# Six eighths of one output store moved from SyncE's queue to GpSimd's, in transfers of 5, 121 and 2 partitions

## The chip, the cores and the metric

The kernel runs on one core of one Trainium2 chip. The metric is the device time of one execution in microseconds, lower being better. Times of a kernel come from repeated runs; a profile is one execution with every instruction and every DMA packet recorded.

## The reference

The computation is a batch of 128 independent matrix products in float32:

```python
b1, b2, m, k, n = 8, 16, 256, 512, 384
x      = np.random.randn(b1, b2, m, k).astype(np.float32)
weight = np.random.randn(b1, b2, k, n).astype(np.float32)
np.matmul(x, weight).astype(np.float32)      # (8, 16, 256, 384)
```

67 MB of x and 101 MB of weights are read, 50 MB of output are written, and nothing is used twice.

## The kernel before

The 128 products are worked off in 32 groups (NG) of four (G). A group is 1024 rows of x, four weight matrices and 1024 rows of output. In SBUF one group's x lies as 128 partitions of R = 8 rows each, so that every partition holds 16 KB that are contiguous in memory; its output lies in the same way, as 128 partitions of 8 rows of 384 float32, 12 KB that are contiguous. Weights of a group are one load of 24 KB for each partition, or two loads of 12 KB in the first four and the last two groups (`is_short`).

There is no scheduler: each engine has its program written out by hand, and semaphores order them.

- SyncE (`on_sync`) issues every DMA, all on one queue: for each group the load of x (`load_x`), the store of the group four earlier (`store`; LAG = 4), and the load of the weights (`load_w`). A load waits until the casts of two groups earlier have freed its buffer, a store until its output is copied (`o_copied`). After the last weights the stores of groups 27 to 31 follow. The store of group 26, the sixth last, is issued between the loads of x and of the weights of group 30.
- VectorE (`on_vector`) casts x to bfloat16 (`cast_x`) and most of the weights (`cast_w`, or `cast_short` in the short groups).
- TensorE (`on_tensor`) transposes x through the identity matrix and multiplies; ScalarE (`on_scalar`) copies the transposes out of PSUM (`evacuate`), casts the rest of the weights, and copies the products out (`copy_out`), four copies to a group (T = 4), into one of four output slots (OS). Before the first copy into a slot it waits for the store of the group four earlier.
- GpSimd (`on_gpsimd`) makes the identity matrix at the start and does nothing else.

The last stores differ in their semaphores: those of groups 28 to 30 count on `o_end`, that of group 31 on `o_fin`. SyncE waits for both at its end. Groups below 28 count on one of two semaphores `o_out`. The last group has its own layout (`is_full`), with packets of 3 KB in its store and 4 KB in its load of x.

In the profile's lines, L118 is the load of x, L135 the load of weights, L157 the store, L171 the cast of x, L184 and L200 the casts of weights in long and short groups, L275 the copy of the products.

Of the kernel before, what the change touches and what calls it, by code (L numbers as in the profile page):

```python
# [12 lines left out]
def kernel(  # L13
# [9 lines left out]
    b1, b2, M, K = x.shape  # L23
    _, _, _, N = weight.shape
# [5 lines left out]
    o_rows = out.rearrange("b1 b2 m n -> (b1 b2 m) n")  # L30
# [10 lines left out]
    G = 4  # L41
    C = P // G
    R = G * M // P
    T = R // 2
    SH, SL = 2, 4
    NG = B // G

    XS, WS, OS = 2, 2, 4
# [3 lines left out]
    LAG = 4  # L52
# [6 lines left out]

    PAD = 12  # L60

    ctx.enter_context(tc.tile_critical(sync_engine=mybir.EngineType.Pool, no_gpsimd_drain=True))  # L62

    def sbuf(name, shape, dtype, n):
        return [
            ctx.enter_context(nc.sbuf_tensor(f"{name}{s}", shape, dtype)) for s in range(n)
        ]
# [6 lines left out]
    def sems(name, n):  # L74
        return [tc.alloc_semaphore(f"{name}{s}") for s in range(n)]
# [9 lines left out]
    out_sb = sbuf("out_sb", [P, OS * R, N], fp32, 1)[0]  # L85
# [6 lines left out]
    id_done, x_cast, w_vcast, w_acast, t_made, t_copied, p_made, o_copied = (  # L92
        sems(name, 1)[0]
        for name in (
            "id_done", "x_cast", "w_vcast", "w_acast",
            "t_made", "t_copied", "p_made", "o_copied",
        )
    )
    x_in, w_in, o_out = sems("x_in", XS), sems("w_in", WS), sems("o_out", 2)
    h_in = sems("h_in", G)  # L100
    o_end = sems("o_end", 1)[0]
    o_fin, spare = sems("o_fin", 1)[0], sems("spare", 1)[0]

    BIAS = 8
# [17 lines left out]
    def is_full(n):  # L123
        return isinstance(n, int) and n == NG - 1
# [17 lines left out]
    def store(e, t, U, s, pieces=1):  # L142
        n = t * U + s
        dram = o_rows[bass.ds(n * (G * M), G * M)].rearrange("(p r) n -> p r n", r=R)
        if is_full(n):
            dram = o_rows[n * G * M : (n + 1) * G * M].rearrange("(i p r) n -> p i r n", i=G, p=P)
        for q in range(pieces):
            rows = slice(q * R // pieces, (q + 1) * R // pieces)
            last = isinstance(n, int) and n >= NG - OS
            if not last and (not isinstance(n, int) or n >= 2):  # L150
                e.wait_ge(o_out[s % 2], (t * (U // 2) + s // 2) * 16 + 16)
            e.wait_ge(o_copied, n * T + ((q + 1) * T // pieces + BIAS))
            src = out_sb[:, bass.ds(slot(t, U, s) * R + q * R // pieces, R // pieces)]
            if is_full(n):
                src = src.rearrange("p (i r) n -> p i r n", i=G)
                rows = slice(0, G)
            e.dma_start(out=dram[:, rows], in_=src).then_inc(  # L157
                o_fin if last and n == NG - 1 else o_end if last else o_out[s % 2], 16
            )

    def slot(t, U, s):
        return (t * U + s) % OS
# [106 lines left out]
    def copy_out(e, t, U, s, q):  # L269
        n = t * U + s  # L270
        if q == 0:
            if not isinstance(n, int) or n >= OS:
                e.wait_ge(o_out[s % 2], (t * (U // 2) + s // 2) * 16 + (16 - OS // 2 * 16 + 16))
        e.wait_ge(p_made, n * T + (q + 1 + BIAS))
        e.copy(  # L275
            out=out_sb[:, bass.ds(slot(t, U, s) * R + 2 * q, 2), :],
            in_=po[(s * T + q) % PO][:, :, :N],
        ).then_inc(o_copied, 1)

    def on_gpsimd(e):  # L280
        e.memset(identity[:], 0.0).then_inc(id_done, 1)  # L281
        e.wait_ge(id_done, 1)
        make_identity(nc, identity[:], nomemset=True)
        e.drain().then_inc(id_done, 1)

    def on_sync(e):
        U = 2
        for n in range(LAG):
            load_x(e, 0, NG, n)
            load_w(e, 0, NG, n)  # L290
        rounds = (NG - 2 - LAG) // U
        with e.Fori(0, rounds) as t:
            for s in range(U):
                load_x(e, t, U, LAG + s)
                store(e, t, U, s)
                load_w(e, t, U, LAG + s)

        for n in range(LAG + rounds * U, NG):
            load_x(e, 0, NG, n)
            if n < NG - 1:  # L300
                store(e, 0, NG, n - LAG)
            load_w(e, 0, NG, n)
        for n in range(NG - 1 - LAG, NG):
            store(e, 0, NG, n)
        e.wait_ge(o_end, 16 * (OS - 1))
        with e.Fori(0, 4):
            e.sem_inc(spare, 1)
        for _ in range(PAD):
            e.sem_inc(spare, 1)
        e.wait_ge(o_fin, 16)  # L310
# [46 lines left out]
    def on_scalar(e):  # L357
# [8 lines left out]
        def step(t, U, s):  # L366
            short = is_short(t * U + s + 1)
            evacuate(e, t, U, s + 1, range(T - 1))
            for q in range(T):
                copy_out(e, t, U, s, q)  # L370
                if q == 0:
                    evacuate(e, t, U, s + 1, range(T - 1, T))
                if q == 0 and short:
                    e.sem_inc(w_acast, CA)
                if q > 0 and not short:
                    last = CA if q == T - 1 else q
                    cast_w(e, t, U, s + 1, range(CV + q - 1, CV + last), q == 1)
# [11 lines left out]
        for q in range(T):  # L389
            copy_out(e, 0, NG, NG - 1, q)  # L390

    on_gpsimd(nc.gpsimd)
    on_sync(nc.sync)
    on_vector(nc.vector)
# [32 lines left out]
```

## Time and profile before

| | before |
|---|---|
| median of 3 runs | 517.65 us (517.05 to 517.83) |
| the profiled execution | 517.57 us |
| its span, first to last instruction | 515.8 us |
| DVE busy | 397.7 us (77%) |
| ACT busy | 409.7 us (79%) |
| PE busy | 320.0 us (62%) |
| POOL busy | 0.7 us (0%) |
| DMA moved | 218.18 MB at a mean of 423 GB/s |
| store of a group | 1536.0 KB, median 25.0 us from issue to landing |

DVE is VectorE, ACT ScalarE, PE TensorE, POOL GpSimd, SP SyncE. The span is cut into 40 slices in the page, and each digit of a row is the busy share of a slice in tenths, 9 standing for 90% or more; the row DMA is the mean over the core's 16 DMA engines. A time from issue to landing includes the queue that stood ahead. In a timeline, a line gives start, length, engine, source line, operation and tiles, the number of instructions, and in brackets the idle time before with what ended it.

### The profile page before, as it was taken

To read this page: it belongs to the slowest core of one execution; us is meant where nothing else is said; L and a number is where in the kernel's file an instruction comes from. 1 tells how busy PE (TensorE), PEld (TensorE's weight loads), DVE (VectorE), ACT (ScalarE), POOL (GpSimd) and SP (SyncE) were. 2 spreads that over 40 slices of the span, in tenths; PEclk is the share of its full clock that TensorE was granted. 3 is DMA by queue.
4 is the path that set the end of the run, shared out by engine and by line. 5 is a ranking of instruction groups with operands and counts; after the bars stand their busy time and mean duration, and the time that the engine had idled before them with its cause. 6 is when DMAs were issued, how large, how long until landed. Compare 5 with 4: busy or idle time off the path is not lost.

```text
span 515.8 us, 11659 instructions
## 1 busy us (share of the span) xinstructions
PE 320.0 (62%) x4512; PEld 222.0 (43%) x4512; DVE 397.7 (77%) x462; ACT 409.7 (79%) x387; POOL 0.7 (0%) x6
## 2 busy tenths in 40 slices
PE   2276737567586656675655864767657477656871
PEld 2254425444354443453443543535445354434550
DVE  2788757788777897777977778877789777797960
ACT  1365577798978997987998799889798978997751
POOL 0000000000000000000000000000000000000000
PEclk9698878677866877876888686778667876877697
DMA  8999999999999999999999999999999999999996
GB/s 337 428 423 426 437 430 420 435 431 433 431 424 432 430 439 428 429 426 432 433 436 428 423 434 431 437 429 425 430 431 434 433 429 427 430 435 423 421 429 250
DMA packets 15462, 218.18 MB, mean 423 GB/s; under 512 B 1632, under 2 KB 1632, under 8 KB 2656
## 3 DMA queue, kind: packets, MB, share of 16 engines
q1 hardware_dynamic: 15456, 218.11, 99.3%
q8 instruction: 3, 0.05, 0.0%
q14 instruction: 3, 0.02, 0.0%
HBM read 167.77 MB, written 50.33 MB: 423 GB/s over the span
## 4 chain that ended last, share of the span: by engine, by line
DMA 57%; DVE 29%; issue 9%; PE 1%; DVEq 1%; SPq 1%; ACT 0%; POOLq 0%
DMA w_sb<-in_weight_dram 57%; DVE w_bf L184 20%; DVE x_bf L171 5%; DVE w_bf L200 4%; PE po L260 1%; SPq L135 0%; DVEq L334 0%; SPq L118 0%; DVEq L62 0%; DVEq L180 0%; ACT out_sb L275 0%; SPq L130 0%; DVEq L168 0%; DVEq L194 0%; SPq L422 0%
## 5 line engine op out<-in xcount | busy, mean ns | idle before, releaser
L184 DVE CAST w_bf<-w_sb 32x1536 bf16<-32x1536 f32 x286 | 271.9, 951 | 81.1 <-DMA w_sb<-in_weight_dram 73.0
L242 PE MATMUL po<-w_bf,x_t 128*32 128x384 bf16 x3968 | 201.5, 364 | 33.4 <-DVE w_bf L184 25.4
L224 PE MATMUL pt<-identity,x_bf 128*128 128x128 f32 x512 | 113.5, 409 | 149.1 <-DVE x_bf L171 149.1
L184 ACT CAST w_bf<-w_sb 32x1536 bf16<-32x1536 f32 x130 | 191.0, 1470 | 5.1 <-DMA w_sb<-in_weight_dram 1.9
L224 PEld LDWEIGHTS pt<-identity,x_bf 128*128 128x128 f32 x512 | 101.3, 223 | 161.5 <-issue 161.0
L242 PEld LDWEIGHTS po<-w_bf,x_t 128*32 128x32 bf16 x3968 | 117.7, 107 | 116.3 <-issue 51.5
L275 ACT COPY out_sb<-po 128x768 f32 (+1 forms) x128 | 102.5, 800 | 59.7 <-PE po L242 53.9
L211 ACT COPY x_t<-pt 128x1024 bf16<-128x1024 bf16 x128 | 123.6, 1021 | 20.9 <-PE pt L224 20.3
L171 DVE CAST x_bf<-x_sb 128x1024 bf16<-128x1024 f32 x128 | 80.0, 688 | 12.5 <-DMA x_sb<-in_x_dram 11.7
L200 DVE CAST w_bf<-w_sb 64x1536 bf16<-64x1536 f32 x48 | 45.8, 955 | 8.3 <-DMA w_sb<-in_weight_dram 7.0
L211 ACT ACT_TABLE_LOAD x1 | 1.3, 1283 | 10.8 <-PE pt L224 10.8
L260 PE MATMUL po<-w_bf,x_t 128*128 128x384 bf16 x32 | 5.4, 326 | 2.8 <-DVE w_bf L200 2.8
L260 PEld LDWEIGHTS po<-w_bf,x_t 128*128 128x128 bf16 x32 | 3.1, 98 | 5.1 <-issue 3.1
masks.py:199 POOL TENSOR_SCALAR_AFFINE_SELECT identity<-identity 128x128 f32<-128x128 f32 x1 | 0.3, 294 | 0.2 <-POOL identity L281 0.2
L281 POOL MEMSET identity<- 128x128 f32 x1 | 0.2, 205 | 0.5 <-POOLq L62 0.5
L411 POOL MEMSET const-bfloat16-1.0<- 128x1 bf16 x1 | 0.1, 102 | 0.0
L411 POOL MEMSET const-uint8-127<- 128x1 uint8 x1 | 0.1, 102 | 0.0
L411 POOL MEMSET const-float32-0.0<- 128x1 f32 x1 | 0.1, 99 | 0.2 <-issue 0.2
L411 POOL MEMSET const-float32-1.0<- 128x1 f32 x1 | 0.1, 99 | 0.0
## 6 DMA issues: line engine op xcount, KB each, us to landing
w_sb<-in_weight_dram SPq DMA_DIRECT2D x26, 3072.0 KB, 18.2
x_sb<-in_x_dram SPq DMA_DIRECT2D x32, 2048.0 KB, 22.3
out_dram<-out_sb SPq DMA_DIRECT2D x32, 1536.0 KB, 25.0
w_sb<-in_weight_dram SPq DMA_DIRECT2D x12, 1536.0 KB, 16.7
```

Of the source, the lines that this page charges most:

```text
L171: e.tensor_copy(out=x_bf[s % BS][:, rows].rearrange("p r (s q c) -> p r s q c", s=S, c=KO), in_=x_sb[s % XS][:, rows].rearrange("p r (q s ...
L184: copy(out=w_bf[(s * G + i) % WBS][h * C : (h + 1) * C], in_=w_sb[s % WS][i * C : (i + 1) * C, h * KO : (h + 1) * KO, :],).then_inc(w_vcas ...
L200: e.tensor_copy(out=w_bf[(n * G + d * SH + a) % WBS][h * p : (h + 1) * p], in_=w_sb[n % WS][a * p : (a + 1) * p, r : r + KO, :],).then_inc ...
L211: e.copy(out=x_t[s % TS][:, 2 * q : 2 * q + 2], in_=pt[(s * T + q) % PT][:].bitcast(bf16),).then_inc(t_copied, 1)
L224: ins = e.transpose(pt[(s * T + q) % PT][:, rr, h, :], words[:, 2 * q + rr, h :: KO // 2], identity[:],)
L242: ins = e.matmul(po[(s * T + q) % PO][mine, rr, :N], x_t[s % TS][:, 2 * q + rr, ko // 2, mine, ko % 2], w_bf[(s * G + i) % WBS][:, ko, :], ...
L260: ins = e.matmul(po[(s * T + q) % PO][:, rr, :N], x_t[s % TS][:, 2 * q + rr, ko // 2, :, ko % 2], w_bf[(s * G + q) % WBS][:, ko, :], start ...
L275: e.copy(out=out_sb[:, bass.ds(slot(t, U, s) * R + 2 * q, 2), :], in_=po[(s * T + q) % PO][:, :, :N],).then_inc(o_copied, 1)
L281: e.memset(identity[:], 0.0).then_inc(id_done, 1)
L411: nc = _bacc.Bacc("TRN2", target_bir_lowering=False, num_devices=1)
```

## The change

For group 26 (`SHARED = NG - 2 - LAG`) alone, SyncE's store writes only the first two (`HR`) of each partition's eight rows, 3 KB for each of 128 partitions, at its old place in the queue. GpSimd writes the other six rows (`store_rest`): after its identity it waits for the group's last output copy, resets the cursor with which its transfers take DMA engines, and issues three transfers, of partitions 0 to 4, 5 to 125, and 126 to 127. Each partition's 9 KB are cut into two elements of 4,608 B. The three transfers count on a semaphore of their own, `rest_out`, and `copy_out` of group 30, which reuses the slot, waits for all of them in addition to SyncE's store. The bytes moved stay the same. Other instructions keep their order on every engine.

```diff
+    SHARED, HR = NG - 2 - LAG, 2
...
+    rest_out = sems("rest_out", 1)[0]
...
             src = out_sb[:, bass.ds(slot(t, U, s) * R + q * R // pieces, R // pieces)]
+            if is_shared(n):
+                rows = slice(0, HR)
+                src = src[:, rows]
             if is_full(n):
...
+    def store_rest(e):
+        n = SHARED
+        e.wait_ge(o_copied, n * T + T + BIAS)
+        e.inc_swdge_sem([], [], mode="reset_dge_cursor")
+        dram = o_rows[n * G * M : (n + 1) * G * M].rearrange("(p r) n -> p r n", r=R)
+        a = slot(0, NG, n) * R
+        p = 0
+        for k in (5, 121, 2):
+            e.dma_start(
+                out=dram[p : p + k, HR:],
+                in_=out_sb[p : p + k, a + HR : a + R],
+                max_dma_last_dim=(R - HR) // 2 * N * 4,
+            ).then_inc(rest_out, 16)
+            p += k
+
+    def is_shared(n):
+        return isinstance(n, int) and n == SHARED
...
         if q == 0:
             if not isinstance(n, int) or n >= OS:
                 e.wait_ge(o_out[s % 2], (t * (U // 2) + s // 2) * 16 + (16 - OS // 2 * 16 + 16))
+            if isinstance(n, int) and is_shared(n - OS):
+                e.wait_ge(rest_out, 16 * 3)
...
         e.drain().then_inc(id_done, 1)
+        store_rest(e)
```

## The prediction

> **What bounds the kernel now.** I read the slices of the page first, then the DMA queues, then the tail of the execution in windows of one microsecond, and last VectorE's timeline ahead of the end. From the page:
>
> ```profile
> DMA  8999999999999999999999999999999999999996
> GB/s 337 428 423 426 437 430 420 435 431 433 431 424 432 430 439 428 429 426 432 433 436 428 423 434 431 437 429 425 430 431 434 433 429 427 430 435 423 421 429 250
> q1 hardware_dynamic: 15456, 218.11, 99.3%
> ```
>
> All 16 DMA engines are busy from the second slice to the last but one, at 420 to 439 GB/s, while VectorE has 77% and ScalarE 79% of the span. All traffic is on one queue, SyncE's. The bytes don't change with the edit, so it can win only through how the bytes lie on the 16 engines, or in the tail. The tail, in columns time, PE, PEld, DVE, ACT, POOL, clock, DMA share, GB/s:
>
> ```profile
> 506.00:507.00 1.00, 0.00 (x0) 0.00 (x0) 0.00 (x0) 0.11 (x1) 0.00 (x0) 1.00 0.50 209
> 507.00:508.00 1.00, 0.00 (x0) 0.00 (x0) 0.00 (x0) 0.00 (x0) 0.00 (x0) 1.00 0.97 393
> 510.00:511.00 1.00, 0.00 (x0) 0.00 (x0) 0.00 (x0) 0.00 (x0) 0.00 (x0) 0.50 1.00 393
> 511.00:512.00 1.00, 0.00 (x0) 0.00 (x0) 0.00 (x0) 0.00 (x0) 0.00 (x0) 0.50 0.23 89
> 512.00:513.00 1.00, 0.00 (x0) 0.00 (x0) 0.00 (x0) 0.00 (x0) 0.00 (x0) 0.50 0.07 28
> 513.00:514.00 1.00, 0.00 (x0) 0.00 (x0) 0.00 (x0) 0.00 (x0) 0.00 (x0) 0.50 0.07 27
> ```
>
> A share of 0.07 is one engine of 16. So nearly all engines have written the last store by 511.2, and one alone works on until 513.8. At 506 to 507 half of the engine time is idle: most engines wait there for the last store to be issued, while the late ones still write the store before.
>
> The packet records say more. The trace doesn't number the engines, but each packet starts 3 or 4 ns before its engine's last one ends, and every engine gets the same sizes in the same order. So the 15,456 packets fall into 16 chains of 966 (two chains that meet within a few ns could be swapped). When store 30 ends (505.9 us on the earliest chain) the chains are late by 0, 0.05, 0.26, 0.36, 0.44, 0.45, 0.60, 0.65, 0.70, 0.89, 1.08, and then **1.37, 1.96, 2.04, 2.49 and 4.08 us**. Where does the lateness come from? Three chains carry one 16 KB instruction fetch each (1028 to 1098 ns, between 15 and 44 us) and two an 8 KB one (309 and 316 ns, at 58 and 71 us); each is put back by 0.7 us or more, for good (they are those of 2.49, 2.04, 1.96, 1.37 and 1.08). The 4.08 us chain has none of those: its packets last 5 to 8 ns longer than the others' again and again (465 for 460, 619 for 611, 920 for 912) and eighteen of them 60 to 90 ns longer; it falls back by some 0.2 us in each 31.6 us. A landing needs the last of 16 chains, so late chains delay every load; at the end they delay the span itself.
>
> **What the change does, part by part.** *Spread of store 26.* Now each chain gets 8 packets of 12,288 B. Start to start a packet takes 456.5 ns (460 less the overlap of 3.5), so 3.65 us. After it, SyncE's part is 8 packets of 3,072 B (121 ns in store 31, so 117.5): 0.94 us per chain. GpSimd's part is two packets of 4,608 B for each partition. No packet of that size is in the trace. Between its neighbours, 159 ns for 4,096 B and 460 for 12,288, it lies at 178, start to start 174; at the rate of 12,288 B it would be 171, at that of 3,072 B 176, so this hardly matters.
>
> Which chain gets which partitions is the disputed cost. Rows show only 128 partitions, 8 to each of 16 chains. For 121 the bounds are: 7 or 8 on each (even), 11 on each of 11, or all on one. I take 11 on each of 11, because 121 is 11 times 11, because 5 and 11 make 16, and because the cursor is reset just ahead: the 5 partitions go to the first five engines, the 121 to the other eleven, and the last 2 wrap to the first two. Then:
> - eleven engines: 22 x 0.174 + 0.94 = 4.77 us, **1.12 us more** than 3.65;
> - three engines: 2 x 0.174 + 0.94 = 1.29, **2.36 us less**; two engines: 4 x 0.174 + 0.94 = 1.64, **2.01 less**.
>
> If the five relieved engines are the five latest chains, the latest chain ends store 30 at 4.08 - 2.36 = 1.72 us (2.07 if it gets two partitions), and the latest of the eleven at 1.08 + 1.12 = 2.20. The last engine then reaches store 31 at 505.9 + 2.2 = 508.1 instead of 510.0: **1.88 us earlier**. Store 31 itself (32 x 117.5 ns = 3.8 us) and what follows are unchanged.
>
> On the numbering, the trace is silent. [...]
>
> *Earlier start and the path to the last store.* GpSimd waits for the fourth copy of group 26 alone, which ends at 443.1 (442.31 + 0.78), where SyncE issued at 449.73:
>
> ```profile
> 442.31 0.78 ACT L275 COPY out_sb<-po 128x768 f32 x1
> ```
>
> ```profile
> 449.73 0.39 SPq L157 DMA_DIRECT2D out_dram<-out_sb  x1
> ```
>
> Nothing is queued on GpSimd behind the wait: its identity is done at the start (0.7 us busy in all). Its three issues and the reset are absent from the trace; even at ten times SyncE's 0.39 us for each issue they end by 460, and only copy_out of group 30 needs the store done, which makes its first copy at 493.1 (L275). So that added wait costs nothing; with that cover gone it would cost what lies beyond 493. The rest store now shares the engines with weight load 29, behind which it used to stand. On the eleven engines all 3.8 us may come ahead of that load: 462.9 + 1.06 + 3.8 = 467.8, against 466.4 now, a landing 1.4 us later at the most (nothing at the least). VectorE waits for it and then runs without a break:
>
> ```profile
> 461.52 2.91 DVE L184 CAST w_bf<-w_sb 32x1536 bf16<-32x1536 f32 x3
> 466.99 7.83 DVE L184 CAST w_bf<-w_sb 32x1536 bf16<-32x1536 f32 x8 [2.55 <-DMA w_sb<-in_weight_dram]
> 474.85 2.50 DVE L171 CAST x_bf<-x_sb 128x1024 bf16<-128x1024 f32 x4
> 477.38 2.91 DVE L184 CAST w_bf<-w_sb 32x1536 bf16<-32x1536 f32 x3
> 480.32 7.86 DVE L200 CAST w_bf<-w_sb 64x1536 bf16<-64x1536 f32 x8
> 488.21 2.50 DVE L171 CAST x_bf<-x_sb 128x1024 bf16<-128x1024 f32 x4
> 491.81 7.86 DVE L200 CAST w_bf<-w_sb 64x1536 bf16<-64x1536 f32 x8 [1.09 <-DMA w_sb<-in_weight_dram]
> ```
>
> Of the 1.4 us the idle 1.09 takes most: the last casts start between 490.7 and 492.1 instead of at 491.81 (the late weights themselves land earlier, at 487.6 + 2.2 = 489.8). So store 31, issued at 506.13 with its first packet at 507.06, moves by -1.1 to +0.4 and could start by 507.5, still ahead of 508.1. I charge nothing; the cover is 0.6 us. Weight load 31, issued at 480.32, may come 1.4 us later too, but load x31 keeps the engines busy until 483.9 or later.
>
> *The rest.* SyncE issues as many instructions as before, with a smaller store. ScalarE has one more wait. Both cost nothing by the above.
>
> **The rivals.** *A: the worst chain is one of the eleven.* Then it gets 11 partitions and ends 1.12 us later than now, at 5.20: 517.57 + 1.12 = 518.7, slower. It decides from the ninth partition on that engine. For it: no row numbers the chains, six chains, not five, carry a fetch or the drift, and a random place gives 11 in 16. Against it: the fetches serve a few instruction streams, which makes neighbouring places for the late chains plausible, and the lateness takes its first larger steps at the fifth and fourth (1.08, 1.37, 1.96). [...]
>
> *B: even spread.* Each chain gets 8 x (2 x 0.174 + 0.1175) = 3.73 us, 0.08 more: 517.6, no change. Against it speaks that a transfer of 5 partitions and one of 2 cannot be laid evenly on 16 chains at all.
>
> *C: the worst chain is relieved but one of the next is not.* 2.49 + 1.12 = 3.61 against 4.08: 517.1, within 0.2%.
>
> *D: 121 partitions on one engine.* 242 x 0.174 = 42 us on one chain, which delays the loads: about 555.
>
> **How the numbers follow.** The profiled execution took 517.57 us (span 515.8 and 1.8 around it), 0.08 from the median of 517.65. The forecast is 517.65 - 1.88 = 515.8, chance 0.54. A has 0.28, B 0.07, C 0.08, D 0.03. The gain can't pass the issue of store 31: 510.0 - 507.5 = 2.5 us, so 515.1, and less 0.1 for runs that differ 515.0 is the lower end. The upper end takes in A with the spread of runs (0.2): 518.9. For the forecast alone the range is 515.0 to 516.5. Faster or slower by over 0.2% is over 1.04 us, about what a measurement of this kernel can tell from no change. Faster: the forecast and a little of C, 0.55. Same: B, most of C, and 0.04 of A, which lies just past the bound: 0.18. Slower: the rest of A and D, 0.27.
>
> **What would show it.** In the profile after, GpSimd's queue holds 256 packets of 4,608 B from 445 to 470 us; 22 of them lie in each of eleven chains. Right: the windows after 509 lose the stretch of 0.07, the share falls at once from near 1 to 0, and the five chains that were latest end store 30 by 508. The step on the path is right if VectorE's wait ahead of its last eight casts shrinks and store 31 is issued between 505.0 and 506.5. Wrong by A: the stretch of 0.07 gets 1.1 us longer. Wrong by B: 16 chains get 16 packets each. The forecast fails also if store 31 is issued after 507.2, since then casts, matmuls and copies set the end, and not the engines.

## The result, and the profile after

| | before | after |
|---|---|---|
| median | 517.65 us (517.05 to 517.84, 6 runs) | 520.51 us (520.27 to 520.72, 6 runs) |
| the profiled execution | 517.57 us | 520.48 us |
| its span | 515.8 us | 518.7 us |
| POOL busy | 0.7 us | 3.0 us |
| first transfer of weight load 31 issued | 480.32 us | 484.60 us |
| store 31 issued | 506.13 us | 509.23 us |

The ratio is 1.0056 (95% interval 1.0043 to 1.0069): 2.9 us slower. The forecast was 1.9 us faster, and the time lies above the range as well. In the page after, the same rows as before, with the new queue (q0 is GpSimd's):

```profile
DMA  8999999999999999999999999999999999999996
GB/s 334 430 425 426 429 433 424 434 432 432 435 425 427 431 435 437 425 422 434 432 431 431 431 428 431 433 437 428 424 431 432 442 423 430 424 419 418 372 390 266
q1 hardware_dynamic: 15456, 216.93, 98.5%
q0 software_dynamic: 464, 1.18, 0.6%
```

In the lines of the changed kernel L138 is the load of weights, L163 SyncE's store, L175 GpSimd's, L195 the cast of x, L208 and L224 the casts of weights, L301 the copy of the products.

Up to the 35th slice the rates are much as before; the 36th and 37th, in which the moved store now lies, are a little lower (419 and 418 GB/s for 435 and 423). Most of the loss shows in the 38th and 39th, 372 and 390 GB/s where 421 and 429 stood: 480 to 506 us, behind the moved store, whose last packet ends at 465.5. The digits alone (9 and 9) do not show it. VectorE's timeline, in the lines that answer to those of before:

```profile
461.68 2.91 DVE L208 CAST w_bf<-w_sb 32x1536 bf16<-32x1536 f32 x3
471.28 7.82 DVE L208 CAST w_bf<-w_sb 32x1536 bf16<-32x1536 f32 x8 [6.69 <-DMA w_sb<-in_weight_dram]
479.13 2.50 DVE L195 CAST x_bf<-x_sb 128x1024 bf16<-128x1024 f32 x4
481.66 2.91 DVE L208 CAST w_bf<-w_sb 32x1536 bf16<-32x1536 f32 x3
484.61 7.86 DVE L224 CAST w_bf<-w_sb 64x1536 bf16<-64x1536 f32 x8
492.50 2.50 DVE L195 CAST x_bf<-x_sb 128x1024 bf16<-128x1024 f32 x4
494.92 7.85 DVE L224 CAST w_bf<-w_sb 64x1536 bf16<-64x1536 f32 x8
```

The wait for weight load 29 is 6.69 us instead of 2.55: the load's last chain lands at 471.2 instead of 466.9. From there on VectorE never stops, and the 1.09 us of idle time that it had before the last casts are used up; those begin 3.1 us late. GpSimd and SyncE:

```profile
442.08 2.36 POOL L175 DMA_DIRECT2D out_dram<-out_sb  x3 [440.35 <-ACT out_sb L301]
484.60 0.81 SPq L138 DMA_DIRECT2D w_sb<-in_weight_dram  x2
509.23 0.39 SPq L163 DMA_DIRECT2D out_dram<-out_sb  x1
```

GpSimd issues three transfers in 2.36 us, right after the last copy of group 26. SyncE issues the first half of weight load 31 4.3 us late, since it waits for VectorE's casts to free the buffer, and store 31 3.1 us late. What the engines do meanwhile, in the windows of after, columns as in the prediction:

```profile
482.00:483.00 1.00, 1.00 (x6) 1.00 (x5) 0.97 (x2) 1.00 (x3) 0.00 (x0) 0.50 0.91 373
484.00:485.00 1.00, 0.15 (x4) 0.15 (x8) 0.97 (x2) 0.02 (x1) 0.00 (x0) 1.00 0.73 299
493.00:494.00 1.00, 0.67 (x4) 0.68 (x5) 1.00 (x3) 0.00 (x0) 0.00 (x0) 0.76 1.00 209
515.00:516.00 1.00, 0.00 (x0) 0.00 (x0) 0.00 (x0) 0.00 (x0) 0.00 (x0) 0.50 0.08 31
516.00:517.00 1.00, 0.00 (x0) 0.00 (x0) 0.00 (x0) 0.00 (x0) 0.00 (x0) 0.50 0.08 30
```

and the same three microseconds before:

```profile
482.00:483.00 1.00, 1.00 (x16) 0.54 (x12) 0.97 (x2) 0.00 (x0) 0.00 (x0) 0.50 1.01 401
484.00:485.00 1.00, 1.00 (x20) 0.60 (x16) 0.97 (x2) 1.00 (x2) 0.00 (x0) 0.55 1.05 430
493.00:494.00 1.00, 1.00 (x33) 0.63 (x24) 0.97 (x2) 0.89 (x2) 0.00 (x0) 1.00 1.04 442
```

Two different losses stand here. At 482 to 487 the share falls to 0.91 and 0.73: the first engines have finished load x31 at 482.0 and 482.9 and have nothing to do, as load 31 isn't issued before 484.60. At 493 the share is 1.00 but the rate half: the engines are busy with packets that take long. The packet records say how long: those of 12,288 B, 460 to 463 ns on average before, take 600 to 940 ns on average in each microsecond from 491 to 495, up to 1,566. Last, the stretch of one engine of 16 (0.08) at the end is still there, only later.

The packet records of the moved store itself show what the prediction took for it: 256 packets of 4,608 B between 446.2 and 465.5, 249 of them of 178 ns, 22 on each of eleven chains, 4, 4, 2, 2, 2 on five. Counted from weight load 26 to the first half of load 30 a loaded chain takes 60.77 us for 59.64 before (+1.13; 1.12 worked out) and a relieved one 57.41 (-2.23; 2.36 worked out). The drifting chain, that of 4.08 us before, is one of the five. The three chains with a 16 KB fetch are not. In these records the packets of the two queues take turns on an engine, as a rule one of GpSimd's and one of SyncE's, and GpSimd's store, issued at 442.08, has its first packet at 446.2, while SyncE's store 25, issued at 434.10, has its first at 452.4: it doesn't wait for what SyncE had queued ahead of it.

A third thing had not been foreseen. Between 454 and 461 us store 25, on SyncE's queue, and GpSimd's store run at once, and five chains have slow packets there: up to 1,509 ns for 12,288 B. A chain with a 16 KB fetch, 1.9 us late in this run, loses 2.1 us to them and is from then on the latest.

### The profile page after: what moved, and what is told of

It reads as the page before. It is cut to its first block, busy times and chain, and to the rows that moved or that the text cites. A ratio compares the mean times of both kernels' runs of the same rounds, so it can differ in the third digit from the quotient of the medians.

```text
span 518.7 us, 11663 instructions
## 1 busy us (share of the span) xinstructions
PE 311.8 (60%) x4512; PEld 221.0 (43%) x4512; DVE 397.7 (77%) x462; ACT 409.8 (79%) x387; POOL 3.0 (1%) x9
## 2 busy tenths in 40 slices
DMA packets 15926, 218.18 MB, mean 421 GB/s; under 512 B 1840, under 2 KB 1840, under 8 KB 3248
## 3 DMA queue, kind: packets, MB, share of 16 engines
q1 hardware_dynamic: 15456, 216.93, 98.5%
## 4 chain that ended last, share of the span: by engine, by line
DMA 58%; DVE 29%; issue 9%; PE 1%; DVEq 1%; SPq 0%; ACT 0%; POOLq 0%
DMA w_sb<-in_weight_dram 43%; DVE w_bf L208 19%; DMA x_sb<-in_x_dram 16%; DVE x_bf L195 7%; DVE w_bf L224 3%; PE po L284 1%; DVEq L361 0%; DVEq L64 0%; SPq L138 0%; DVEq L204 0%; ACT out_sb L301 0%; DVEq L192 0%; SPq L133 0%; SPq L121 0%; SPq L449 0%
## 5 line engine op out<-in xcount | busy, mean ns | idle before, releaser
L208 DVE CAST w_bf<-w_sb 32x1536 bf16<-32x1536 f32 x286 | 271.8, 950 | 85.2 <-DMA w_sb<-in_weight_dram 77.1
L266 PE MATMUL po<-w_bf,x_t 128*32 128x384 bf16 x3968 | 193.3, 353 | 35.0 <-DVE w_bf L208 25.1
L208 ACT CAST w_bf<-w_sb 32x1536 bf16<-32x1536 f32 x130 | 191.0, 1469 | 7.7 <-DMA w_sb<-in_weight_dram 4.6
L248 PEld LDWEIGHTS pt<-identity,x_bf 128*128 128x128 f32 x512 | 102.8, 224 | 173.0 <-issue 172.8
L266 PEld LDWEIGHTS po<-w_bf,x_t 128*32 128x32 bf16 x3968 | 115.1, 104 | 111.3 <-issue 46.8
L301 ACT COPY out_sb<-po 128x768 f32 (+1 forms) x128 | 102.4, 800 | 56.0 <-PE po L266 52.1
L195 DVE CAST x_bf<-x_sb 128x1024 bf16<-128x1024 f32 x128 | 80.1, 690 | 12.4 <-DMA x_sb<-in_x_dram 11.6
L224 DVE CAST w_bf<-w_sb 64x1536 bf16<-64x1536 f32 x48 | 45.8, 955 | 7.4 <-DMA w_sb<-in_weight_dram 6.1
L175 POOL DMA_DIRECT2D out_dram<-out_sb x3 | 2.4, 788 | 440.4 <-ACT out_sb L301 440.4
```

Source lines behind the costliest of these rows:

```text
L175: e.dma_start(out=dram[p : p + k, HR:], in_=out_sb[p : p + k, a + HR : a + R], max_dma_last_dim=(R - HR) // 2 * N * 4,).then_inc(rest_out, 16)
L195: e.tensor_copy(out=x_bf[s % BS][:, rows].rearrange("p r (s q c) -> p r s q c", s=S, c=KO), in_=x_sb[s % XS][:, rows].rearrange("p r (q s ...
L208: copy(out=w_bf[(s * G + i) % WBS][h * C : (h + 1) * C], in_=w_sb[s % WS][i * C : (i + 1) * C, h * KO : (h + 1) * KO, :],).then_inc(w_vcas ...
L224: e.tensor_copy(out=w_bf[(n * G + d * SH + a) % WBS][h * p : (h + 1) * p], in_=w_sb[n % WS][a * p : (a + 1) * p, r : r + KO, :],).then_inc ...
L248: ins = e.transpose(pt[(s * T + q) % PT][:, rr, h, :], words[:, 2 * q + rr, h :: KO // 2], identity[:],)
L266: ins = e.matmul(po[(s * T + q) % PO][mine, rr, :N], x_t[s % TS][:, 2 * q + rr, ko // 2, mine, ko % 2], w_bf[(s * G + i) % WBS][:, ko, :], ...
```

## The experiments

Two theories stood after this. By the first the **start** is at fault: GpSimd's packets no longer wait for what is queued on SyncE, weight load 29 lands later, and the delay runs on through casts, load 31 and store 31. By the second the **spread** is at fault: eleven engines with 11 partitions each get slow packets and become the bound. All runs are compared with the kernel before on the same chip, whose medians were 517.71 to 517.76 us.

**1. The early start with an even spread** (edit to the changed kernel):

```diff
-        for k in (5, 121, 2):
+        for k in (128,):
...
-                e.wait_ge(rest_out, 16 * 3)
+                e.wait_ge(rest_out, 16)
```

> Theory 1 (the store that jumps ahead of weight load 29 delays VectorE, so weight load 31 is issued late and the DMA queue runs dry): with 128 partitions in one transfer each engine gets 16 packets of 4,608 B, 2.8 us ahead of load 29, so VectorE's wait ahead of its casts is about 5.3 us instead of 2.55, load 31 is issued near 483 instead of 480.3, the queue is dry for under 1 us, and the time is 517.8 to 518.7. Theory 2 (only the uneven spread costs): time 517.7, as before. If the engines share evenly, no chain has more than 16 packets of 4,608 B.

Measured: 519.50 us, ratio 1.0038 (1.0023 to 1.0052). All 16 chains have 16 packets, and none is slow between 446 and 480 us.

```profile
469.93 7.83 DVE L208 CAST w_bf<-w_sb 32x1536 bf16<-32x1536 f32 x8 [4.75 <-DMA w_sb<-in_weight_dram]
```

The wait for load 29 is still 2.2 us longer than before, load 31 is issued at 483.26 and store 31 at 507.89. So three fifths of the loss (519.50 - 517.76 = 1.74 of 2.9 us) need no uneven spread and no slow packets of the store. The packet records say where they go: the latest chain takes 5.5 us for the second half of load 31, where it took 3.7 before. The theory of the start is right in kind, but its price was set too low; that of the spread alone falls.

**2. The uneven spread without the early start** (GpSimd waits until store 25 has landed, so that its packets no longer pass load 29's place by much):

```diff
         e.wait_ge(o_copied, n * T + T + BIAS)
+        e.wait_ge(o_out[1], 224)
         e.inc_swdge_sem([], [], mode="reset_dge_cursor")
```

> GpSimd waits until store 25 has landed. Theory 1a (the slow packets of 454 to 461 us come from store 25 and GpSimd's store reading SBUF at once): no packet between 445 and 480 us takes over 1.2 times its usual time, load 29 lands 2 us earlier than with the change, load 31 is issued by 482.5, the time is 518 to 519. Rival 1b (any traffic of GpSimd's queue beside SyncE's makes slow packets): packets of over 0.8 us for 12,288 B, or of longer than usual for other sizes, still stand beside GpSimd's, and the time stays near 520.5.

Measured: 517.35 us, ratio 0.9991 (0.9981 to 1.0000).

```profile
460.38 3.12 POOL L176 DMA_DIRECT2D out_dram<-out_sb  x3 [458.66 <-DMA out_dram<-out_sb]
467.30 7.82 DVE L209 CAST w_bf<-w_sb 32x1536 bf16<-32x1536 f32 x8 [2.92 <-DMA w_sb<-in_weight_dram]
```

Issued at 460.4 instead of 442.1, the same three transfers cost nothing: the wait for load 29 is 2.92 us, load 31 is issued at 480.62, store 31 at 506.02, about as before. The slow packets at 455 to 469 are gone; a few are left at 470 to 471 (up to 931 ns), just while SyncE's part of store 26 runs, and a few in load 31, at 482 (1,171 and 1,502 ns) and 488 to 492 (up to 681 ns), though not on the latest chain. One wait gives back 3.2 us (520.51 to 517.35), more than was expected of it. Yet the 1.9 us of the forecast don't appear: the interval reaches no change.

**3. The order of the three transfers**, to find out where the late engines are:

```diff
-        for k in (5, 121, 2):
+        for k in (121, 5, 2):
```

> Transfers of 121, 5 and 2 partitions in this order: by the reset cursor the 121 load the first eleven engines and the last five are relieved (and the first two get one more). If the three late chains that carry a 16 KB instruction fetch lie on the last five engines, they are relieved, load 29 lands earlier than with the change and the time is under 519.5. If they lie in the middle, the time is 520 to 521 and the drifting chain ends last, 1.1 us later than before or more.

Measured: 520.85 us, ratio 1.0056 (1.0039 to 1.0073). Now the drifting chain has 22 packets, and the three chains with a 16 KB fetch have 2; in the changed kernel it was 2 and 22. So the drifting chain is one of the five that the transfer of 5 takes when it goes first (with 2 packets in the changed kernel, not 4: one of the three that the last 2 partitions leave out), and the three with the large fetch are among the five that the transfer of 5 takes when it follows the 121. The order 5, 121, 2 relieves the one, the order 121, 5, 2 the three, and neither all four. The expectation was that with the fetches relieved the time would fall below 519.5. They are relieved, and it didn't: the time is that of the changed kernel although other engines are loaded (wait for load 29 6.54 us, load 31 issued at 485.03). Of these two placements, with the early start, neither is better.

**4. Load 31 late by itself** (edit to the kernel before; no store is moved, the load of group 31's weights waits for the fourth of the eight casts of group 30's weights):

```diff
+            else:
+                e.wait_ge(w_vcast, 30 * CV + 7)
```

> The kernel before, with one wait more: SyncE issues weight load 31 only after the fourth cast of weights 30, some 4 us later (about 484.3), as the changed kernel did (484.6). Theory 1 (a dry queue costs more than its idle time, since the engines restart in step and then have slow packets): the share falls at 483 to 486, packets of 12,288 B take 0.6 to 1.5 us in 490 to 495, the time is 519 to 520. Theory 2 (the latest engine never runs dry, so a late issue costs nothing): 517.7, and no slow packets.

Measured: 519.02 us, ratio 1.0023 (1.0014 to 1.0033). Load 31 is issued at 483.95, 3.6 us late, and this alone costs 1.3 us:

```profile
485.00:486.00 1.00, 0.87 (x24) 0.36 (x12) 0.97 (x2) 0.22 (x2) 0.00 (x0) 1.00 0.84 242
493.00:494.00 1.00, 1.00 (x32) 0.67 (x28) 0.97 (x2) 0.11 (x1) 0.00 (x0) 1.00 0.62 209
```

Both losses of the changed kernel are seen here without its store: idle engines and slow packets at 484 to 486 (up to 1,394 ns), and the slow stretch at 491 to 493 (up to 1,182 ns). The latest chain again takes 5.5 us for the second half of load 31 instead of 3.7. So the second half of the chain (late load 31, late end) is shown by itself.

**5. The same, some 1.4 us earlier** (it waits for the second cast instead of the fourth), so that the queue doesn't run dry:

```diff
+            else:
+                e.wait_ge(w_vcast, 30 * CV + 4)
```

> The kernel before, with weight load 31 held back until the second cast of weights 30 (w_vcast over 30 groups plus 4), so issued near 482.2, 2 us late, before the earliest engine has finished load x31 (483.9). Theory (only a queue that has run dry makes slow packets): the share stays near 1 from 480 to 490, no packets of 12,288 B over 0.6 us, time 517.5 to 517.9. Rival (any lateness of that load costs in proportion): 518.2 to 518.5.

Measured: 518.53 us, ratio 1.0013 (1.0003 to 1.0022); the profiled execution, the slowest of the ten, took 519.38. In it load 31 is issued at 482.60, 1.25 us before the first engine reaches it; from 484 to 493 the engines stay at a share of 0.90 to 1.20, and still

```profile
491.00:492.00 1.00, 1.00 (x12) 0.78 (x13) 0.02 (x1) 1.00 (x3) 0.00 (x0) 1.00 1.20 258
```

packets are slow at 484 (up to 1,049 ns) and at 490 to 492 (up to 1,393 ns). The latest chain loses 1.8 us in the second half of load 31, as in experiments 1 and 4. A dry queue as the only price of the lateness falls: load 31, issued 1.25 us before the first engine reached it, costs 0.8 us already. Load 31, which the prediction called covered until 483.9, was not covered at 482.6. (Store 31 is late too in this execution, issued at 509.45: TensorE's granted clock was 0.50 during part of its last matmuls, from 503 to 505 us. It holds most chains until 514.3, but not the latest, which comes to store 31 later and ends at 515.6.)

**6. No store of SyncE beside GpSimd's** (GpSimd stores all eight rows, after store 25; SyncE stores nothing of group 26):

```diff
-    SHARED, HR = NG - 2 - LAG, 2
+    SHARED, HR = NG - 2 - LAG, 0
...
+        e.wait_ge(o_out[1], 224)
...
-            if n < NG - 1:
+            if n < NG - 1 and n - LAG != SHARED:
...
-            if not isinstance(n, int) or n >= OS:
+            if not isinstance(n, int) or (n >= OS and n - OS != SHARED):
```

> GpSimd writes all eight rows of store 26 (packets of 6,144 B), after store 25 has landed, and SyncE no store 26 at all, so no two stores run at once between 460 and 480 us. Theory (packets slow down where two queues read SBUF for stores at once, since GpSimd's engines read other partitions than their own): no packet over 1.2 times its usual time in 460 to 480. Rival (slow packets come from GpSimd's transfers as such): they stay. Loaded engines get 5.0 us, 1.3 more: latest loaded chain 2.49 + 1.3 = 3.8 against 4.08, time 517.3 to 517.9.

Measured: 517.38 us, ratio 0.9993 (0.9983 to 1.0004). The spread is 22 on eleven, 4, 4, 2, 2, 2 on five, and there is no slow packet from 464 to 480. With the even spread (experiment 1) there was none either, with two stores at once. So the slow packets of the stores took both in these runs: an uneven store and a second store at the same time. Why, no record shows: that of a packet has its queue, size and times, but not the partition that it reads. It doesn't cover all: in the changed kernel two packets of load x30 take 874 and 1,092 ns at 471.9, when GpSimd's store is over.

**7. Fewer rows, after store 25** (three rows to GpSimd instead of six, in elements of 2,304 B):

```diff
-    SHARED, HR = NG - 2 - LAG, 2
+    SHARED, HR = NG - 2 - LAG, 5
...
+        e.wait_ge(o_out[1], 224)
...
-                max_dma_last_dim=(R - HR) // 2 * N * 4,
+                max_dma_last_dim=(R - HR) * N * 2,
```

> GpSimd waits until store 25 has landed, and takes three rows instead of six, in packets of 2,304 B (about 89 ns start to start). Eleven engines get 22 x 0.089 + 2.29 = 4.25 us instead of 3.65, 0.6 more; five get 1.2 less. Theory (the drifting chain is among the relieved, the chains with a 16 KB fetch among the loaded): the drifting chain ends store 30 at 4.08 - 1.2 = 2.9, the latest loaded one at 2.49 + 0.6 = 3.1, 1.0 us before the old end: 516.4 to 517.0. Rival (the drifting chain is loaded): 4.08 + 0.6, so 518.3.

Measured: 517.22 us, ratio 0.9989 (0.9980 to 0.9999), 0.5 us faster than before, with an interval that just excludes no change; the expectation was missed by 0.2. It is the lowest median here, but those of experiments 2, 6 and 11 lie within 0.2 us of it and can't be told from it. The two elements of a partition go as one packet of 4,608 B, so a loaded chain has 11.

```profile
491.38 7.86 DVE L225 CAST w_bf<-w_sb 64x1536 bf16<-64x1536 f32 x8 [0.29 <-DMA w_sb<-in_weight_dram]
505.71 0.39 SPq L163 DMA_DIRECT2D out_dram<-out_sb  x1
```

```profile
511.00:512.00 1.00, 0.00 (x0) 0.00 (x0) 0.00 (x0) 0.00 (x0) 0.00 (x0) 0.50 0.39 157
512.00:513.00 1.00, 0.00 (x0) 0.00 (x0) 0.00 (x0) 0.00 (x0) 0.00 (x0) 0.50 0.20 79
513.00:514.00 1.00, 0.00 (x0) 0.00 (x0) 0.00 (x0) 0.00 (x0) 0.00 (x0) 0.50 0.02 6
```

This is the mechanism of the forecast at work: the stretch of 0.07 after 513 is all but gone, and the drifting chain ends at 512.9 instead of 513.8. But at 512 the share is 0.20, three engines of 16, where it was 0.07: the three chains with a large fetch now end at 512.5, 512.5 and 513.3, as the prediction's rival C has it. The last landing of store 31 is 0.82 us earlier (513.72 for 514.54), of which 0.5 us reach the time.

**8. Both kinds of late engines relieved**, after store 25: the transfers above for rows 5 to 7, and row 4 in five transfers that are meant to spare the chains with a large fetch as well.

```diff
+        for r0, r1, ks in ((5, 8, (5, 121, 2)), (4, 5, (3, 102, 5, 13, 5))):
...
-                e.wait_ge(rest_out, 16 * 3)
+                e.wait_ge(rest_out, 16 * 8)
```

> After store 25 has landed GpSimd takes three rows in transfers of 5, 121 and 2 partitions and a fourth in transfers of 3, 102, 5, 13 and 5, by which the sixth to eleventh engine get 17 partitions of that row and the last five few. SyncE keeps four rows (8 packets of 6,144 B, 1.84 us). Drifting chain: 1.84 + 0.18 + 0.13 = 2.15, 1.5 less: 2.6. Chains with a 16 KB fetch, if they lie on the last five: 1.84 + 1.96 + 0.13 = 3.93, 0.3 more: 2.8. The six: 1.84 + 1.96 + 1.2 = 5.0, 1.3 more: 2.2. The end comes 1.3 us earlier: 516.1 to 516.9, faster than with three rows alone. Rival (the 102 do not go to six engines): a chain of more than 18 packets of 768 B, and no gain over three rows.

Measured: 517.62 us, ratio 1.0001 (0.9991 to 1.0010). In the profiled execution the engines do finish earlier: store 31 lands at 513.38, 1.2 us before its time of before. More than half of it is lost again, since the eight transfers cost something at the other end. After the last landing GpSimd runs a drain, and its record is 41 ns without a transfer of GpSimd (the kernel before), 142 with one (experiment 1), 313 with three (the changed kernel) and 722 with eight (this one): 85 to 101 ns for each, on the path. For the changed kernel that is 0.27 us, for this one 0.68. This execution, at 517.03, was the fastest of the ten; why the median lies 0.6 us above it, no trace shows.

**9 and 10. Six engines take the load**, 102 partitions being 6 times 17, after store 25, with three rows and with four:

```diff
-        for k in (5, 121, 2):
+        for k in (5, 102, 21):
```

> Three rows of store 26 go to GpSimd after store 25 has landed, in transfers of 5, 102 and 21 partitions: 102 load the sixth to eleventh engine with 17 partitions each, 21 give three each to the last five and the first two. Theory (the drifting chain is one of the third to fifth engine, the chains with a 16 KB fetch among the last five): drifting chain 2.30 + 0.17 = 2.47 us instead of 3.65, so 4.08 - 1.18 = 2.9; fetch chains 2.30 + 0.52 = 2.82, so 2.49 - 0.83 = 1.7; the six 2.30 + 17 x 0.1745 = 5.27, so 0.9 + 1.62 = 2.5. The last engine ends store 30 1.2 us earlier, GpSimd's drain costs 0.27 more: 516.5 to 517.1. Rival (late chains are not where the order of transfers showed them): 517.5 or more.

> As the kernel of 5, 102 and 21 partitions, with four rows instead of three: drifting chain 4.08 - 1.58 = 2.5, fetch chains 1.4, the six 0.9 + 2.1 = 3.0 us. End 1.1 us earlier, the drain 0.27: 516.6 to 517.2, no better than three rows.

Measured: 518.03 us, ratio 1.0006 (0.9997 to 1.0015), and 517.96 us, ratio 1.0002 (0.9993 to 1.0011). With three rows, six chains have 17 packets, the drifting one has 1 and the three with the large fetch have 3, as wanted: drift and fetches are relieved together. No gain: slow packets are back at 470 to 474 (up to 1,095 ns). The chain that ends last is again the drifting one, at 514.2: it has slow packets there, and the second half of load 31 takes it 4.5 us instead of 3.7. The six end by 512.8. With four rows the six are the latest, and store 31 is issued at 508.38, because TensorE's granted clock is 0.50 from 502 to 505 us in this execution and the last 32 matmuls take 7.04 us instead of 5.36. So its profile doesn't settle what four rows are worth.

**11. Two transfers instead of three** (7 and 121 partitions, three rows, after store 25):

```diff
-        for k in (5, 121, 2):
+        for k in (7, 121):
```

> Three rows after store 25 in two transfers of 7 and 121 partitions: the eleven from the eighth engine on, wrapping to the first two, get 11 partitions, the five between one each. Drifting chain 2.9 as with three transfers, fetch chains 2.49 + 0.6 = 3.1. GpSimd's last drain is 0.09 us shorter than with three transfers (about 225 ns against 313). Time 516.6 to 517.3. Rival (the drifting chain is the first or second engine): it is loaded, 518.3.

Measured: 517.27 us, ratio 0.9991 (0.9982 to 1.0000), as with three. The same drain is 229 ns, in line with its price for each transfer. Five chains have 1 packet, two have 12, nine have 11, and the drifting chain has 1: it is not one of the two that both transfers load, which fits its 2 packets, not 4, in the changed kernel.

## Why the prediction was wrong

*The bound.* Right: engines fully busy (99.3% of their span before, 98.5 and 0.6% on the two queues after), bytes unchanged (218.18 MB), the end set by the latest chains. What experiments 2 and 7 gain lies there.

*The spread of store 26.* Right in every number: packets of 178 ns (249 of 256), 11 partitions on each of eleven engines, +1.13 and -2.23 us for 1.12 and 2.36. The 11 on each of 11 was the author's choice among three, which no run had shown until then; the runs show 121 partitions on eleven chains (the changed kernel), 102 on six and 21 on seven (experiment 9) and 128 on all 16 (experiment 1). So rivals B and D fall as to the spread. Their prices, and A's, left out the early start: experiment 1 has B's spread and takes 519.50 for the 517.6 of the prediction, experiment 3 loads the drifting chain as A does and takes 520.85 for 518.7.

*"The five relieved engines are the five latest chains."* Wrong. The drifting chain was relieved, so rival A falls, but the three chains of 1.96, 2.04 and 2.49 us were loaded: rival C's placement. Rival C by itself gave 517.1; experiment 2, which takes the early start away, gives 517.35. So a gain of 1.9 us was out of reach even with a later start. The neighbouring places that the prediction guessed for the late chains are borne out for the three with a large fetch only, which one transfer of 5 takes together in experiment 3; the drifting chain is taken by that of the changed kernel.

*"Earlier start: I charge nothing."* This step failed and decides the sign. It bounded the later landing of load 29 at 1.4 us from a chain that is 1.06 us late plus all the store's time; 4.3 us were measured. It left out that the chains with the fetches, which land the load, may be among the eleven (another 0.9 to 1.4 us), and that packets got slower where these two stores ran at once (2.1 us on the latest). It then set the cover against 1.4 us, and the cover was that thin: VectorE's idle 1.09 us are gone, and load 31, "covered until 483.9", was issued at 484.60; experiment 5 shows that already 482.60 costs 0.8 us. The prediction's own test, store 31 after 507.2, came out at 509.23, but its consequence was put wrongly: casts and copies don't set the end in place of the engines, the engines lose time too, because load 31 comes late, and the latest of them still sets the end.

*Sum for the latest chain.* It was 1.9 us late, where the one before was 4.08: -2.2. Its partitions add 1.1, the slow packets beside store 25 2.1, those of load 31's second half 2.2: together +3.2, and its last packet of store 30 ends 3.15 us later (513.13 for 509.98). Store 31 then lands 2.69 us later, and the longer drain makes that 2.96; the medians differ by 2.9. Without this one chain the end would still be later than before: the second latest, slowed in the same two places, lands at 515.5, 1.0 us after the last one of before, and since store 31 was issued late, even the first chains end it at 514.1, later than the last did before (513.8).

*What was hidden.* The issues (0.79 us each, for the tenfold 3.9 that the prediction allowed) and the wait of group 30's first copy cost nothing, as stated. The drain at the end was not in the sum.

What stays open: why the packets of load 31's second half, at 490 to 495 us, get slow when its first half was issued late (experiments 4 and 5 show that they do, not why), why packets were slow where the uneven store ran beside another, and why one engine drifts.

## What to carry to other kernels

The part of store 26 that moved to a second queue did not wait for what stood ahead of it in the first one: its first packet came at 446.2, that of the part left on SyncE's queue at 468.7. When a transfer moves like this, list what it passes, add its whole time (and the lateness of the slowest engine that it lands on) to each load behind it, and follow that load's consumers to the next buffer they free. A cover is worth what is left of it when several such terms are added. The uneven transfers took weight off the late DMA engine (2.23 us in the changed kernel), but they paid 0.5 us at most, and only where they were started so late that the next load which VectorE waits for came at most 0.5 us later. Relieving the other late engines too (experiments 8 and 9) brought no lower median.

## What the runs showed of the hardware that was not expected

- Two stores at once, one of them uneven: 12,288 B packets of up to 1,509 ns for 460. None in the stores when both were even (experiment 1), none from 464 to 480 us when the second was left out (experiment 6).
- Load 31, issued 2.3 to 4.3 us late (the changed kernel, experiments 1, 4 and 5), ran slower, also where the engines weren't idle yet (experiment 5): 209 to 258 GB/s for 393 to 442 in the slowest microseconds from 491 to 494, at shares of 0.62 to 1.20. From 493 to 494 the engines moved 209 GB/s at a share of 1.00 in the changed kernel, and 442 at 1.04 in the one before.
- The slow packets in the first half of load 31 went with how soon after its issue the engines reached it. Where the first engines came to load 31 within 2.3 us of its issue (experiments 2, 5, 6, 8 and 11), the longest packet of each run in its first half took 1,049 to 1,789 ns for 460. Where they came 2.5 us after it (7, 9 and 10) there were two slow ones of up to 794 ns or none, and before, 3.55 us after it, none. No run changes this alone.
- GpSimd's drain after the last landing took 142, 229, 313 and 722 ns with one, two, three and eight of its transfers, for 41 with none: 85 to 101 ns more for each.
- Two elements of 2,304 B that lie side by side went as one packet of 4,608 B (experiment 7: 11 packets on a chain with 11 partitions).
- One engine's packets from two queues took turns: between 449 and 463 us the latest chain has 22 of GpSimd's, as a rule with one of SyncE's after each.
